# The input projection by seven products of halves, and attention beside the gates and the convolution's branch

## The chip, the cores and the metric

The kernel runs on one core of one Trainium2 chip. The time is the device time of one launch in microseconds (us), the median of the runs shown. The engines are named as in the profile: PE is TensorE's matmul, PEld its weight load, DVE VectorE, ACT ScalarE, POOL GpSimd, SP the queue that issues nearly all DMAs.

## The reference

One layer of a streaming encoder for 1024 prompt positions and 32 decoded ones, 1056 together, in float32:

```python
h = rmsnorm(x, g_mix);  proj = h @ w_in                     # 1024 -> 5120 columns
q, k, v, cb, cc, cx, ga, gc = split(proj)                   # 512 each; ga and gc 1024 each
z = q @ k.T / 8                                             # 8 heads of 64
a = sigmoid(z) * (product of 1 - sigmoid(z) over the keys between key and query), keys before the query only
y_attn = (a @ v) @ w_attn_out
conv_out = w[0] * u[t-2] + w[1] * u[t-1] + w[2] * u[t]      # u = cc * cx
y_conv = (cb * conv_out) @ w_conv_out
x = x + (sigmoid(ga) * y_attn + sigmoid(gc) * y_conv) @ w_o
x = x + square(relu(rmsnorm(x, g_ffn) @ w_up)) @ w_down
x = x + sigmoid(rmsnorm(x, g_ple) @ w_ple_gate) * (p @ w_ple);  y = rmsnorm(x, g_final)
```

k, v and the last two rows of u are outputs too. The 32 decoded positions attend to 256 cached keys as well.

## The kernel before

Activations lie with 128 features on the partitions and the 1056 positions along the row, 8 blocks of features for 1024. Each float32 operand is split into a high part that the matmul takes as it is (ACT copies it) and the rest (DVE subtracts), and a product is three matmuls: high by high, high by low, low by high (`gemm`, L102 to L108). The weight scale g_mix goes into x before the product, and the mean square of each position comes later: `rs`, one factor per position, multiplies each result of the input projection.

**The input projection** is 40 blocks of 128 columns. Each block is 3 tiles of 352 positions, and a tile ("group", one bank of PSUM) is 8 blocks of features by 3 matmuls of 352 columns. `first_unit` makes the blocks q0, k0 and v0 while x arrives, `qkv_unit`, `gate_unit` and `conv_unit` the others. `run_units` hands them out group by group.

**Attention** goes in 64 steps (p, j, i): 8 heads, and for each a round of 8 blocks of 128 queries; step i has i + 1 blocks of keys. Four stages of one step run in consecutive steps: `scores` (z on PE, two sigmoids on ACT, and on POOL a select that masks the last block of `r` and of `s`, L459), `weigh` (a running product over `r` on DVE, L467, and a multiply into `s`, L468), `flip` (transposes `pa` on PE, high part on ACT, low part on DVE, L498), `gather` (`av` on PE, L515, added on DVE, L523). Between these stages `fill` lets PE work on groups of the input projection: FILL of them in a round, spread by the number of keys of a step. In this part the order on each engine is the framework's scheduler's. Other parts (`tc.manual_schedule`) keep the order of the code.

**After attention** come the 12 blocks of the convolution (`conv_unit`), then 8 units of the convolution's branch ("oc"), 8 of attention's branch ("oa"), each 3 groups of 12 matmuls of 352, then 8 of w_o, and the MLP. A branch unit loads its gate from DRAM (`gd`), takes the sigmoid on ACT and multiplies it into the product as DVE reads it from PSUM; POOL adds the two branches (L666).

**w_up and w_down already go by seven products.** With two blocks of output columns, even and odd blocks of features and two halves of the positions, a product is a 2 by 2 matrix of blocks: weights A11 to A22, activations B11 to B22. Seven products of halves and sums of operands (S1 to S4 of the weights, T1 to T4 of the activations) take the place of eight. A "set" of w_up is two blocks of columns: 7 products x 2 quarters of 264 positions x 4 blocks of features x 3 matmuls = 168 matmuls of 264 columns, where two blocks by `gemm` are 2 x 3 x 8 x 3 = 144 matmuls of 352. POOL forms the sums of weights, and `run` and `side` interleave such steps with the products. w_up's code in line: `prepare_up`, `products` (L889 to L891), `up_set`.

SBUF has one pool of 34 tiles of a whole row (`blk`) for nearly everything.

## Time and profile before

| | us |
|---|---|
| median of 3 runs (1603.44 to 1609.71) | 1607.92 |
| the profiled execution: its own time | 1604.31 |
| its span, first to last instruction | 1602.6 |
| PE busy | 1564.4 (98%) |
| DVE busy | 996.3 (62%) |
| ACT busy | 671.0 (42%) |
| POOL busy | 328.1 (20%) |

The mean granted clock of PE is 0.993. Stages in the trace, from the span's start: the first matmul at 6.6 us, attention's first scores at 62.3 and its last `av` at 464.3, the convolution's branch from 596.6, attention's branch from 643.0, w_o from 689.3, w_up from 782.2, w_down from 1120.6, the last stage from 1478.0. A matmul's row gives a duration that overlaps with the next matmul's, so the cost of one in a dense stretch is the stretch's busy time over its count.

### The profile page before, as it was taken

How to read it: one execution, taken by the hardware profiler on the slowest of the kernel's cores; microseconds unless marked ns; L12 is line 12 of the kernel's file. 1: busy time of each engine (PE TensorE's matmuls, PEld its weight loads, DVE VectorE, ACT ScalarE, POOL GpSimd, SP SyncE). 2: the span in 40 equal slices, each digit the busy share in tenths (PEclk: the TensorE clock that was granted, in tenths of full speed). 3: DMA queues.
4: the chain of work that ended last, by engine and by line, in shares of the span. 5: the costliest groups of instructions: out<-in, count | busy, mean ns of one | idle time of the engine just before them, and what ended most of it. 6: DMA issues, size and time to landing. Idle time of an engine off the chain costs nothing.

```text
span 1602.6 us, 27656 instructions
## 1 busy us (share of the span) xinstructions
PE 1564.4 (98%) x11154; PEld 1547.2 (97%) x11154; DVE 996.3 (62%) x1386; ACT 671.0 (42%) x1105; POOL 328.1 (20%) x380
## 2 busy tenths in 40 slices
PE   8999999999999999999999999999999999998996
PEld 8999999999989999999989999999899999998996
DVE  4567676776544444565576555554478958897546
ACT  7344343444331114433355555555343344344443
POOL 0112222222220000321222222220011301022423
PEclk9999999999999999999999999999999999999998
DMA  7533242423111117433444443435877977752123
GB/s 309 192 97 117 74 143 76 124 95 100 61 67 42 39 33 250 161 120 127 149 169 148 148 147 134 144 141 189 292 259 234 312 253 232 244 181 80 50 80 135
DMA packets 99792, 238.39 MB, mean 149 GB/s; under 512 B 11824, under 2 KB 25776, under 8 KB 99664
## 3 DMA queue, kind: packets, MB, share of 16 engines
q1 hardware_dynamic: 99520, 236.60, 43.4%
q8 instruction: 87, 1.43, 0.4%
q14 instruction: 41, 0.34, 0.1%
q10 hardware_dynamic: 144, 0.03, 0.0%
HBM read 168.72 MB, written 63.68 MB: 145 GB/s over the span
## 4 chain that ended last, share of the span: by engine, by line
PE 80%; issue 6%; DVE 6%; DMA 2%; ACT 2%; POOL 2%; SPq 1%; POOLq 0%; DVEq 0%; ACTq 0%
PE ps_dn L1162 5%; PE ps_dn L1160 5%; PE ps_dn L1161 5%; PE ps_A L890 4%; PE ps_A L891 4%; PE ps_A L889 4%; PE ps_g L108 3%; PE ps_g L107 3%; PE ps_g L106 3%; PE ps_wo L107 2%; PE ps_wo L106 2%; PE ps_wo L108 2%; PE av L515 2%; PE ps_pg L106 2%; PE ps_S L890 2%
## 5 line engine op out<-in xcount | busy, mean ns | idle before, releaser
L1162 PE MATMUL ps_dn<-fh,wlo_dn 128*128 128x264 f32 x896 | 256.1, 286 | 3.3 <-DVE wlo_dn L1040 3.3
L1160 PE MATMUL ps_dn<-fh,whi_dn 128*128 128x264 f32 x896 | 255.9, 286 | 3.0 <-ACT whi_dn L1034 3.0
L1161 PE MATMUL ps_dn<-fl,whi_dn 128*128 128x264 f32 x896 | 255.3, 285 | 0.0
L1162 PEld LDWEIGHTS ps_dn<-fh,wlo_dn 128*128 128x128 f32 x896 | 169.3, 189 | 4.1 <-DVE wlo_dn L1040 4.1
L1160 PEld LDWEIGHTS ps_dn<-fh,whi_dn 128*128 128x128 f32 x896 | 169.4, 189 | 3.2 <-ACT whi_dn L1034 3.2
L1161 PEld LDWEIGHTS ps_dn<-fl,whi_dn 128*128 128x128 f32 x896 | 169.5, 189 | 0.0
L106 PE MATMUL ps_g<-xh,whi_g 128*128 128x352 f32 x384 | 127.3, 331 | 0.0
L107 PE MATMUL ps_g<-xl,whi_g 128*128 128x352 f32 x384 | 124.6, 324 | 0.0
L108 PE MATMUL ps_g<-xh,wlo_g 128*128 128x352 f32 x384 | 124.4, 324 | 0.0
L467 DVE TENSOR_TENSOR_SCAN r<-r 128x128 f32<-128x128 f32 (+3 forms) x64 | 87.6, 1370 | 34.9 <-POOL r L459 34.4
L1040 DVE TENSOR_TENSOR wlo_dn<-raw_dn,whi_dn 128x1024 fp32r<-128x1024 f32 x40 | 69.7, 1742 | 25.3 <-ACT whi_dn L1034 25.1
L876 POOL TENSOR_TENSOR s<-raw_u,raw_u 128x512 f32<-128x512 f32 x30 | 44.1, 1469 | 187.7 <-DVE slS L836 186.9
L451 ACT ACTIVATE r<-z 128x128 f32<-128x128 f32 (+3 forms) x64 | 41.9, 655 | 89.1 <-PE z L446 82.7
L1094 POOL TENSOR_TENSOR c<-c,rs 128x528 f32<-128x528 f32 x16 | 26.7, 1669 | 252.9 <-DVE c L1169 123.0
L1062 DVE TENSOR_TENSOR fl<-mr,fh 128x1056 fp32r<-128x1056 f32 x56 | 69.8, 1247 | 12.3 <-ACT fh L1057 12.3
L1034 ACT CAST whi_dn<-raw_dn 128x1024 fp32r<-128x1024 f32 x40 | 42.0, 1050 | 79.0 <-PE ps_dn L1161 78.6
L106 PEld LDWEIGHTS ps_g<-xh,whi_g 128*128 128x128 f32 x384 | 72.3, 188 | 0.3
L107 PEld LDWEIGHTS ps_g<-xl,whi_g 128*128 128x128 f32 x384 | 72.4, 189 | 0.0
L108 PEld LDWEIGHTS ps_g<-xh,wlo_g 128*128 128x128 f32 x384 | 72.2, 188 | 0.0
L890 PE MATMUL ps_A<-T,shS 128*128 128x264 f32 x240 | 68.4, 285 | 1.7 <-DVE T L776 1.7
L891 PE MATMUL ps_A<-T,slS 128*128 128x264 f32 x240 | 68.4, 285 | 0.0
L889 PE MATMUL ps_A<-B,whi_up 128*128 128x264 f32 x240 | 68.3, 285 | 0.0
(406 smaller groups left out, 4975.3 us busy)
## 6 DMA issues: line engine op xcount, KB each, us to landing
raw_dn<-in_w_down_dram SPq DMA_DIRECT2D x56, 512.0 KB, 4.5
mr<-mdT SPq DMA_DIRECT2D x32, 528.0 KB, 5.4
raw_u<-in_w_up_dram SPq DMA_DIRECT2D x32, 512.0 KB, 3.5
mdB<-m SPq DMA_DIRECT2D x48, 264.0 KB, 2.4
mr<-mdB SPq DMA_DIRECT2D x24, 528.0 KB, 6.0
gd<-sg SPq DMA_DIRECT2D x16, 528.0 KB, 2.7
mdT<-ta SPq DMA_DIRECT2D x32, 264.0 KB, 2.1
raw_g<-in_w_in_dram SPq DMA_DIRECT2D x16, 512.0 KB, 3.9
```

What stands on the lines that cost most here:

```text
L106: nc.tensor.matmul(ps, wh, xh[k][:, cols], start=(k == order[0]), stop=False)
L107: nc.tensor.matmul(ps, wh, xl[k][:, cols], start=False, stop=False)
L108: nc.tensor.matmul(ps, wl, xh[k][:, cols], start=False, stop=(k == order[-1]))
L467: nc.vector.tensor_tensor_scan(rev, rev, rev, 1.0, ALU.mult, ALU.bypass)
L889: nc.tensor.matmul(p_, wh[:, k, :], o[:, 0, c], start=new and n == 0, stop=False, **on)
L890: nc.tensor.matmul(p_, wh[:, k, :], o[:, 1, c], start=False, stop=False, **on)
L891: nc.tensor.matmul(p_, wl[:, k, :], o[:, 0, c], start=False, stop=z, **on)
L1040: dve(lo, raw, hi.bitcast(F32), op=sub)
L1062: dve(l, mraw.pop(v), opd[v].bitcast(F32), op=sub)
L1160: nc.tensor.matmul(ps, hi[:, j, :], oh, start=j == 0, stop=False)
L1161: nc.tensor.matmul(ps, hi[:, j, :], ol, start=False, stop=False)
L1162: nc.tensor.matmul(ps, lo[:, j, :], oh, start=False, stop=j == NP_ - 1)
```

## The change

The input projection goes first, as 14 "sets" of two blocks and 12 single gates. Sets 0 and 1 (4 gates) are plain products, made while x arrives (`first_gates`): 8 products of halves, in quarters of 264. The other 12 sets (cc, cx, cb, q, k, v, blocks 0 and 1; then q, k, v, cc, cx, cb, blocks 2 and 3) go by `seven`, now shared with w_up. `parts_x` and `sums_x` make B11 to B22 and T1 to T4 of the scaled x; `prepare` makes the weights' sums for the next set. What DVE did to a group as it read PSUM (times `rs`) is a step behind the set: `follow` starts generators that scale (`scaled`), split, transpose, convolve and write to DRAM while the next set's products run. Queries, keys, values and the convolution's result now all go through DRAM (`qd`, `kd`, `vd`, `cvd`); `keys_values` loads keys and values for a round one round ahead.

Then attention runs. Its `fill` is now 12 gates (groups of 24 matmuls of 264) and after them the convolution's branch (groups of 12 matmuls of 352), 7.25 groups in a round and not 9.6. A gate leaves PSUM by ACT, unscaled; when a branch unit loads it, POOL multiplies it by `rs` (`branch_unit`, L783 in the changed kernel), ahead of the sigmoid. POOL's addition of the two branches moves to DVE. The decoded positions' attention moves from behind the last step to steps 3, 6 and 9. Behind attention stands what is left of the convolution's branch, attention's branch and w_o as before.

```diff
-GATES = (3, 3, 3, 7)
-FILL = 9.6
+AT_IN = (4, 8, 10, 12, 14, 18)
+PLAIN_GATES = 4
+FILL = 7.25
 FILL_BASE = 2.0
 ORDER = "SAFLBFG"
-START = 9
+START = 6
...
+    def seven(s_, m1, m2, last, after=None):
...
+        for t, a, b in q:
+            x[t] = product("A11", "B11", t)
+            nc.scalar.copy(p1[t], x[t])
+            yield
+        for t, a, b in q:
+            z[t] = product("S1", "T1", t)
+            nc.scalar.copy(s5[t], z[t])
+            yield
+        for t, a, b in q:
+            product("S2", "T2", t, x[t])
+            nc.scalar.copy(u2[t], x[t])
+            yield
+        for t, a, b in q:
+            dve(m1[:, a], product("A12", "B21", t), p1[t], op=add)
+            yield
+        done("11")
+        for t, a, b in q:
+            product("S3", "T3", t, x[t])
+            dve(m2[:, b], x[t], s5[t], op=sub)
+            yield
+        done("22")
+        for t, a, b in q:
+            product("S4", "B22", t, z[t])
+            dve(m1[:, b], u2[t], z[t], op=sub)
+            yield
+        done("12")
+        for t, a, b in q:
+            product("A22", "T4", t, x[t])
+            last(m2, a, x[t])
+            yield
+            if t == 0:
+                done("near")
+        done("21")
...
+    SETS = [("g", 0), ("g", 2)] + [(nm, 0) for nm in ("cc", "cx", "cb", "q", "k", "v")]
+    SETS += [(nm, 2) for nm in ("q", "k", "v", "cc", "cx", "cb")]
+    base = {"g": goff, "q": 0, "k": 4, "v": 8, "cb": coff, "cc": coff + 4, "cx": coff + 8}
...
-    first_raw = {"q": raw_w(w_in, 0, KD, "q0")}
-    load_x(0)
-    first_raw["k"] = raw_w(w_in, 4, KD, "k0")
-    load_x(1)
-    load_x(2)
+    near_, far_, whole_ = slice(0, TQ), slice(TQ, TH), slice(0, TH)
+    n_ = base["g"]
+    raws["i0"] = [raw_w(w_in, n_, KD, "i0_0")]
+    load_x(0, near_)
+    raws["i0"].append(raw_w(w_in, n_ + 1, KD, "i0_1"))
+    load_x(0, far_)
+    load_x(1, whole_)
...
+    def keys_or_queries(nm, p, m):
+        scaled(m, HD**-0.5 if nm == "q" else None)
+        yield
+        d = [qd[p, :, i, :] if nm == "q" else kd[p, i] for i in range(2)]
+        h = blk(f"{nm}h{p}", F32R, [P, SEQ])
+        nc.scalar.copy(h, m[:, :SEQ])
+        nc.scalar.copy((qsT if nm == "q" else ksT)[p], m[:, SEQ:])
+        nc.sync.dma_start(d[0], h.bitcast(F32))
+        if nm == "k":
+            nc.sync.dma_start(k_out[p], m)
+            for _ in range(4):
+                yield
+        yield
+        l = m[:, :SEQ]
+        dve(l.bitcast(F32R), l, h.bitcast(F32), op=sub)
+        nc.sync.dma_start(d[1], l)
...
+            nc.sync.dma_start(vd[p, j], vs.bitcast(F32).rearrange("p a c -> p (a c)"))
...
+    def scaled(m, by=None):
+        if by is None:
+            dve(m, m, rs, op=ALU.mult)
+        else:
+            nc.vector.scalar_tensor_tensor(m, m, by, rs, op0=ALU.mult, op1=ALU.mult)
...
+    def conv_in(nb, m):
+
+        scaled(m)
+        yield
+        u = cst["cc", nb]
+        dve(u, u, m, op=ALU.mult)
...
+        y = cst["y", nb] = blk(f"yc{nb}")
+        nc.scalar.activation(y, u, AF.Copy, scale=w2)
...
+        mix(y[:, 1:], u[:, : T - 1], w1, y[:, 1:], add)
...
+    def conv_gate(nb, m):
+        scaled(m)
+        yield
+        dve(m, m, cst.pop(("y", nb)), op=ALU.mult)
+        yield
+        h = blk(f"cvh{nb}", F32R)
+        nc.scalar.copy(h, m)
+        nc.sync.dma_start(cvd[nb, 0], h.bitcast(F32))
+        yield
+        dve(m.bitcast(F32R), m, h.bitcast(F32), op=sub)
+        nc.sync.dma_start(cvd[nb, 1], m)
...
+    def follow(nm, n, ms, wait=0):
+        gens = []
+        for p, m in zip((n, n + 1), ms):
+            if nm in "qk":
+                gens.append(keys_or_queries(nm, p, m))
+            elif nm == "v":
+                gens.append(values(p, m))
+            elif nm == "cc":
+                cst["cc", p] = m
+                gens.append(call(scaled, m))
+            else:
+                gens.append({"cx": conv_in, "cb": conv_gate}[nm](p, m))
...
-                nc.vector.tensor_tensor(sg[:, ts[t]], ps, rs[:, ts[t]], op=ALU.mult)
+    def gate_group(n, w, sg, t):
+        c = t // 2 + 1
+        ps = products(f"g{n}_{t}", ((w[0], f"B1{c}"), (w[1], f"B2{c}")), quarters[t % 2])
+        nc.scalar.copy(sg[:, quarters[t]], ps)
...
+    def keys_values(p, j):
+        kk = st["k", p, j] = blk(f"ks{p}{j}", F32R, [P, SEQ])
+        for i in range(2):
+            nc.sync.dma_start(kk[64 * i : 64 * i + 64, :].bitcast(F32), kd[p, i, 64 * j : 64 * j + 64, :])
+        vv = st["v", p, j] = blk(f"vv{p}{j}", F32R, [P, 8, P])
+        nc.sync.dma_start(vv.bitcast(F32).rearrange("p a c -> p (a c)"), vd[p, j])
...
     def branch_unit(nm, n, ww, bh, bl):
         def load():
             sg = blk(f"s{nm}{n}")
-            return sg, load_w(ww, n, 4, f"o{nm}{n}")
+            nc.sync.dma_start(sg, gd[n + (8 if nm == "c" else 0)])
+            w = load_w(ww, n, 4, f"o{nm}{n}")
+            pool(sg, sg, rs, op=ALU.mult)
+            nc.scalar.activation(sg, sg, AF.Sigmoid)
...
             if nm == "a" and not last:
-                nc.gpsimd.tensor_tensor(m, m, sg, op=ALU.add)
+                dve(m, m, sg, op=add)
...
-    units = [first_unit()]
-    g_of = GATES
-    g = 0
-    for p in range(4):
-        units += [gate_unit(n) for n in range(g, g + g_of[p])]
-        g += g_of[p]
-        if p < 3:
-            units += [qkv_unit(p + 1, nm) for nm in "qkv"]
-    units += [gate_unit(n) for n in range(g, 16)]
-    units += [conv_unit(nb, nm) for nb in range(4) for nm in ("cc", "cx", "cb")]
-    work = run_units(units, 1)
+    units = [gate_unit(n) for n in range(PLAIN_GATES, 14)] + [last_gates(14)]
+    units += [branch_unit("c", n, w_conv_out, ch, cl) for n in range(KD)]
+    work = run_units(units)
...
+        run(first_gates())
+        for s_ in range(2, len(SETS)):
+            nm, n = SETS[s_]
+            if s_ == 2:
+                side.append(after(1, stats_x()))
+            if s_ + 1 < len(SETS):
+                side.append(prepare(f"i{s_ + 1}", AT_IN))
+            else:
+                side.extend([after(4, second_parts(0)), after(6, second_parts(1)), after(7, call(next, work))])
+            if s_ + 2 < len(SETS):
+                side.append(after(5, call(fetch_in, s_ + 2)))
+            m = blk(f"m1_i{s_}"), blk(f"m2_i{s_}")
+            run(seven(f"i{s_}", *m, copy_of))
+            follow(nm, n, m, 6 * (s_ == 2))
+        keys_values(0, 0)
+        run(ahead(START))
...
-    units = [branch_unit("c", n, w_conv_out, ch, cl) for n in range(KD)]
     units += [branch_unit("a", n, w_attn_out, oh, ol) for n in range(KD)]
     units += [wo_unit(n) for n in range(KD)]
-    run_all(units)
```

How the order moved, at three places. On DVE, what belongs to the convolution's inputs. Before, in the stretch behind attention (`ps_cx`, `ps_cb`: groups in PSUM; `u`: cc times cx; `yc`: the convolution's sum; `wlo_cc`: the next block's weights' low part):

```order
L389 TENSOR_TENSOR cx_5559<-ps_cx_0_5560,rs 128x352
L389 TENSOR_TENSOR cx_5559<-ps_cx_1_5586,rs 128x352
L389 TENSOR_TENSOR cx_5559<-ps_cx_2_5612,rs 128x352
L399 TENSOR_TENSOR u_5638<-cc_5474,cx_5559 128x1024
L400 TENSOR_TENSOR u_5638<-cc_5474,cx_5559 128x32
L98 TENSOR_TENSOR wlo_cc_5653<-raw_cc_5650,whi_cc_5652 128x1024
L407 SCALAR_TENSOR_TENSOR yc_5646<-u_5638,vecT,yc_5646 128x1058
L389 TENSOR_TENSOR cb_5656<-ps_cb_0_5657,rs 128x352
```

Now, in the set of cb behind that of cx (`m_i`: results of a set, `slS`: a weights' sum's low part for the next set, `ps_A12i`, `ps_A11i`: products):

```order
L454 TENSOR_TENSOR m_i_1020<-m_i_1020,rs 128x1056
L239 TENSOR_TENSOR m_i_1287<-ps_A12i_1_1431,p_i_1290 128x264
L505 TENSOR_TENSOR m_i_761<-m_i_761,m_i_1020 128x1056
L244 TENSOR_TENSOR m_i_1288<-ps_A11i_0_1295,s_i_1293 128x264
L153 TENSOR_TENSOR slS_i_1470<-raw_i_1_1165,shS_i_1468 128x512
L244 TENSOR_TENSOR m_i_1288<-ps_A11i_1_1318,s_i_1294 128x264
L142 SCALAR_TENSOR_TENSOR yc_1463<-m_i_761,vecT,yc_1463 128x1055
```

The scaling of a whole row, the convolution and the weights' low parts now stand between the reads of PSUM.

On DVE in attention. Before, at the end of a round and the start of the next (`sg<-ps_g`: a gate leaves PSUM; the running product over `r` is printed here as SCALAR_TENSOR_TENSOR):

```order
L498 TENSOR_TENSOR at_2724<-pa_2827,at_2723 128x2x128
L468 TENSOR_TENSOR s_2810<-s_2810,r_2811 128x1023
L366 TENSOR_TENSOR sg_2838<-ps_g_0_2839,rs 128x352
L467 SCALAR_TENSOR_TENSOR r_2873<-r_2873 128x128
L468 TENSOR_TENSOR s_2872<-s_2872,r_2873 128x127
L498 TENSOR_TENSOR at_2881<-pa_2884,at_2880 128x4x128
```

Now, in a round of the last two heads:

```order
L700 SCALAR_TENSOR_TENSOR r_7356<-r_7356 128x1024
L758 TENSOR_TENSOR oT_7237<-av_7338,avl_7347 64x256
L731 TENSOR_TENSOR at_7295<-pa_7363,at_7294 128x4x128
L801 TENSOR_TENSOR mg_7315<-ps_oc_1_7370,sc_7162 128x352
L701 TENSOR_TENSOR s_7355<-s_7355,r_7356 128x1023
L731 TENSOR_TENSOR at_7297<-pa_7386,at_7296 128x2x128
L801 TENSOR_TENSOR mg_7315<-ps_oc_2_7391,sc_7162 128x352
L99 TENSOR_TENSOR wlo_oc_7489<-raw_oc_7486,whi_oc_7488 128x512
```

In the last two heads' rounds DVE reads the branch's groups, which before stood behind attention; in the earlier rounds it reads no group at all, since ACT does.

On POOL in the same part of attention. Before, selects and memsets alone:

```order
L459 AFFINE_SELECT r_4921<-r_4921 128x128
L459 AFFINE_SELECT s_4920<-s_4920 128x128
L504 MEMSET at_4931 128x128
L459 AFFINE_SELECT r_5025<-r_5025 128x128
L459 AFFINE_SELECT s_5024<-s_5024 128x128
```

Now, with the gates' multiply by `rs` between them (`sc`: a gate loaded for the convolution's branch):

```order
L692 AFFINE_SELECT r_7356<-r_7356 128x128
L692 AFFINE_SELECT s_7355<-s_7355 128x128
L783 TENSOR_TENSOR sc_7305<-sc_7305,rs 128x1056
L692 AFFINE_SELECT r_7413<-r_7413 128x128
L692 AFFINE_SELECT s_7412<-s_7412 128x128
L737 MEMSET at_7422 128x128
L737 MEMSET at_7423 128x128
L692 AFFINE_SELECT r_7461<-r_7461 128x128
L692 AFFINE_SELECT s_7460<-s_7460 128x128
L737 MEMSET at_7524 128x128
L783 TENSOR_TENSOR sc_7484<-sc_7484,rs 128x1056
```

Seven of the sixteen multiplies stand between selects of the last three rounds, the others behind them.

More of the change, by code (lines that the diff above doesn't have):

```diff
@@ new lines, in products @@
+    def products(name, terms, c, p_=None):
+        new = p_ is None
+        if new:
+            p_ = group(f"ps_{name}", TQ)
+        n = 0
+        for (wh, wl), b in terms:
+            for k in range(4):
+                o, z = oper[b][k], n == 4 * len(terms) - 1
+                on = dict(skip_group_check=not new)
+                nc.tensor.matmul(p_, wh[:, k, :], o[:, 0, c], start=new and n == 0, stop=False, **on)
+                nc.tensor.matmul(p_, wh[:, k, :], o[:, 1, c], start=False, stop=False, **on)
+                nc.tensor.matmul(p_, wl[:, k, :], o[:, 0, c], start=False, stop=z, **on)
+                n += 1
+        return p_
@@ new lines, in after, with call, run @@
+    def after(n, *gens):
+        for _ in range(n):
+            yield
+        for g in gens:
+            yield from g
+    def call(f, *a):
+        f(*a)
+        yield
+    def run(body):
+        for _ in body:
+            for g in list(side):
+                if next(g, g) is g:
+                    side.remove(g)
+    goff = (3 * SB + 3 * CW) // P
+    coff = 3 * SB // P
+    SETS = [("g", 0), ("g", 2)] + [(nm, 0) for nm in ("cc", "cx", "cb", "q", "k", "v")]
+    SETS += [(nm, 2) for nm in ("q", "k", "v", "cc", "cx", "cb")]
@@ L697, in row_rms @@
+    for p in range(4):
+        h, l = split(oT[p], f"o{p}")
+        oh.append(h)
+        ol.append(l)
+    c_att.close()
+    gps2 = ctx.enter_context(tc.tile_pool(name="gps2", bufs=4, space=PSUM))
+    c_mlp = ExitStack()
+    fpool = wpool[0] = c_mlp.enter_context(tc.tile_pool(name="fpool", bufs=2))
+    pools[:] = [gps2, gps, gps2]
     def row_rms(src, r9, blocks, name, square=False):
@@ L1488 @@
     data = {
[L1489 removed]
+        "xf": x.T.reshape(KD, P, T),
         "xr_": x,
```

855 lines of the change are left out of this document (407 added, 448 removed).

## The prediction

> **What bounds the kernel now.** I began with the page's busy shares over 40 slices, to see which engine has no slack.
>
> ```profile
> PE   8999999999999999999999999999999999998996
> DVE  4567676776544444565576555554478958897546
> POOL 0112222222220000321222222220011301022423
> PEclk9999999999999999999999999999999999999998
> ```
>
> PE is full from the second slice on, at the full granted clock; DVE has a third to a half of each slice free, POOL more. Then the stretches by windows (the columns are the stretch in us, its length, then busy time and instructions of PE, PEld, DVE, ACT and POOL, the granted clock, the DMA share and GB/s): attention, attention's branch, and some 15 sets of w_up.
>
> ```profile
> 62.00:464.00 402.00, 398.94 (x2621) 388.70 (x2621) 268.08 (x377) 161.09 (x295) 96.19 (x197) 1.00 0.32 103
> 643.00:689.00 46.00, 46.00 (x288) 46.00 (x287) 24.44 (x38) 19.07 (x21) 18.79 (x7) 1.00 0.46 155
> 806.00:1110.00 304.00, 300.85 (x2458) 299.78 (x2457) 171.46 (x254) 165.39 (x317) 76.85 (x56) 1.00 0.43 152
> ```
>
> Attention idles PE for 402.00 - 398.94 = 3.1 us, attention's branch not at all, w_up for 3.2 of 304. PE's waits name what little is lost:
>
> ```profile
> PE ps_q L106 <- ACT xh L161: 6.6, 1, 6.6
> PE ps_A L890 <- DVE T L776: 1.7, 1, 1.7
> PE pas L602 <- DVE ss L468: 1.7, 1, 1.7
> ```
>
> The largest is the program's start. So the time is PE's work, and a change is worth the PE time it removes, less the idle time it opens. For the price of a matmul I also read the starts of two stages of equal matmuls (minimum, median and maximum duration, then first and last start):
>
> ```profile
> L106 PE MATMUL ps_oa<-o0h,whi_oa x24: 322/323/323, 643.0 to 687.4; 128*128 128x352 f32 x24
> L106 PE MATMUL ps_wo<-mh,whi_wo x192: 318/323/330, 689.3 to 781.8; 128*128 128x352 f32 x192
> ```
>
> A matmul of 352 columns costs (689.3 - 643.0) / 288 = 160.8 ns, one of 264 columns, by the window of w_up, 300.85 / 2458 = 122.4 ns.
>
> **The change part by part.** *Products.* Two blocks of queries, keys, values or convolution inputs cost 144 x 0.1608 = 23.16 us now, a set 168 x 0.1224 = 20.56. That is -2.59, and 12 sets give **-31.1**. The 16 gates stay plain but go in quarters: two of them are 192 x 0.1224 = 23.50 for 23.16, +0.35, and 8 pairs give **+2.8**. Sum for PE: -28.3.
>
> The Trainium skill, "TensorE: Matmul & The Clock Gate", section "Back-to-back issue gap", has a rule against all of this: a sustained stream spaces matmuls of 128 columns about 81 ns apart and of 512 about 131, so narrow ones pay a large fixed part. An estimate on its straight line is 99 ns for 264 columns and 110 for 352, and the sum would be about +33, not -28. The trace disagrees with it (122.4 and 160.8, in dense stretches), and the rows decide.
>
> *The start* is plain products as before, in smaller loads of x: the first wait of 6.6 stays, and later parts may come a little sooner or later. Between -1 and +3; I take 0.
>
> *Work behind a set.* A group was scaled as DVE read it from PSUM; now a whole row is scaled in SBUF, split and convolved while the next set runs. The fullest set is that of cb, behind cx. Its rows:
>
> ```profile
> L836 DVE TENSOR_TENSOR slS<-s,shS 128x512 fp32r<-128x512 f32 x45 | 33.6, 746 | 39.7 <-ACT shS L834 39.7
> L98 DVE TENSOR_TENSOR wlo_up<-raw_u,whi_up 128x1024 fp32r<-128x1024 f32 x16 | 19.4, 1214 | 2.4 <-ACT whi_up L97 2.4
> L959 DVE TENSOR_TENSOR m<-ps_A,p 128x264 f32<-128x264 f32 x29 | 12.4, 428 | 16.0 <-PE ps_A L891 16.0
> L632 DVE TENSOR_TENSOR ml<-mg,mh 128x1056 fp32r<-128x1056 f32 x7 | 8.8, 1258 | 15.7 <-ACT mh L631 15.7
> L407 DVE SCALAR_TENSOR_TENSOR yc<-u,vecT,yc 128x1058 f32<-128x1058 f32 x6 | 7.9, 1316 | 1.7 <-ACT yc L405 1.7
> ```
>
> DVE: 6 reads of PSUM x 0.43, 5 low parts x about 0.7 and one of 1.2 for the next set's weights, 2 scalings and 2 products for u at 1.26 each by the row `ml`, 4 passes of the convolution x 1.32, small ones 0.7: 18.3 of PE's 20.56. In w_up it was 171.46 / 15 = 11.4 a set, with 3.15 / 15 = 0.2 us of PE idle each. Sets behind q, k, v need 12 to 14. There are two cx sets and two cb sets; only these are near the limit, and POOL's sums of weights (below) can push them over: 0 to +8, I take **+1.5**.
>
> *DVE and POOL hold each other up.* The timeline and the groups:
>
> ```profile
> 300.62 1.79 POOL L459 TENSOR_SCALAR_AFFINE_SELECT s<-s 128x128 f32<-128x128 f32 x1 [0.62 <-ACT s L451]
> 300.03 2.29 DVE L467 TENSOR_TENSOR_SCAN r<-r 128x1024 f32<-128x1024 f32 x1
> ...
> 854.30 1.63 POOL L876 TENSOR_TENSOR s<-raw_u,raw_u 128x512 f32<-128x512 f32 x1 [0.69 <-DVE slS L836]
> 854.81 1.69 DVE L907 TENSOR_TENSOR m<-m,m 128x528 f32<-128x528 f32 x1
> ...
> L459 POOL TENSOR_SCALAR_AFFINE_SELECT s<-s 128x128 f32<-128x128 f32 x64 | 63.0, 984 | 20.7 <-ACT s L451 20.4
> L459 POOL TENSOR_SCALAR_AFFINE_SELECT r<-r 128x128 f32<-128x128 f32 x64 | 22.6, 354 | 219.8 <-ACT r L451 216.6 <-DMA raw_k<-in_w_in_dram 3.0
> L666 POOL TENSOR_TENSOR mg<-mg,sa 128x1056 f32<-128x1056 f32 x7 | 20.0, 2854 | 116.4 <-DVE sa L660 113.0 <-ACT sa L645 3.4
> L876 POOL TENSOR_TENSOR s<-raw_u,raw_u 128x512 f32<-128x512 f32 x30 | 44.1, 1469 | 187.7 <-DVE slS L836 186.9 <-DMA raw_u<-in_w_up_dram 0.7
> ```
>
> The same select takes 0.29 us beside an idle DVE (r mean 354) and 1.79 beside a scan, ending as the scan does; a DVE operation of 0.7 us takes 1.69 beside a POOL sum and ends 0.57 after it. So a POOL operation of two rows in SBUF costs DVE its time, and the reverse. The change puts 16 such operations in (a gate times `rs`, 128x1056, 2.85 us by L666): 7 among the last rounds' selects, one behind them and 8 in attention's branch; it takes out 7 additions from there.
>
> The Trainium skill says so in "SBUF — State Buffer", section "SBUF: two separate sides": the shared ports are a lock held for a whole instruction. The trace agrees (1.79 against 0.29). By this rule each multiply stops DVE's two-input work entirely; that is the second rival below, and I count a part of it here.
>
> *Attention.* The rows of PE and DVE there, and below the dots two of the branches, which now come in part under it:
>
> ```profile
> L494 PE MATMUL pa<-ident,s 128*128 128x128 f32 x288 | 46.6, 275 | 1.1 <-POOL at L504 0.8 <-POOL s L459 0.3
> L515 PE MATMUL av<-at,vs 128*128 128x256 f32 x316 | 43.5, 284 | 0.9 <-DVE at L498 0.9
> L445 PE MATMUL z<-ks,q 128*128 128x384 f32 (+4 forms) x96 | 33.1, 347 | 0.0
> L446 PE MATMUL z<-ks,q 128*128 128x384 f32 (+4 forms) x96 | 32.9, 344 | 0.9 <-DMA q<-qd 0.9
> L467 DVE TENSOR_TENSOR_SCAN r<-r 128x128 f32<-128x128 f32 (+3 forms) x64 | 87.6, 1370 | 34.9 <-POOL r L459 34.4
> L498 DVE TENSOR_TENSOR at<-pa,at 128x512 fp32r<-128x512 f32 (+2 forms) x96 | 50.8, 542 | 1.4 <-ACT at L497 1.3
> L468 DVE TENSOR_TENSOR s<-s,r 128x127 f32<-128x127 f32 (+3 forms) x64 | 48.1, 753 | 3.0 <-POOL s L459 0.9
> L523 DVE TENSOR_TENSOR oT<-av,avl 64x256 f32<-64x256 f32 x31 | 12.8, 414 | 15.9 <-ACT avl L522 15.6
> ...
> L658 DVE TENSOR_TENSOR mg<-ps_oc,sc 128x352 f32<-128x352 f32 x24 | 12.0, 520 | 10.2 <-PE ps_oc L108 7.3 <-ACT sc L645 3.0
> L98 DVE TENSOR_TENSOR wlo_oa<-raw_oa,whi_oa 128x512 fp32r<-128x512 f32 x8 | 5.5, 684 | 0.0
> ```
>
> Attention's own are 796 matmuls (and 27 of values, moved); the other 1798 of 2621 are input blocks at 0.1608, which leaves 398.94 - 289.1 = 109.8 us, 13.7 a round. DVE's own rows sum to 199.3, at most 24.9 a round. A round had 9.6 x 24 x 0.1608 = 37.0 of other products, 50.7 in all: DVE had slack twice over. A round of gates now has 7.25 x 24 x 0.1224 = 21.3, so 35.0, against DVE's 24.9 plus two low parts of weights of 1.21, 27.3: still PE's, at 78%. In the round that has the convolution's branch alone it is 7.25 x 12 x 0.1608 = 14.0, so 27.7, while DVE has 24.9 + 7.25 x 0.52 (its reads of PSUM) + 2.4 x 0.69 (low parts of the units' weights) = 30.4: 2.7 us over without the multiplies, 10 with 2.6 of them (7 in 2.7 rounds). The last round has the units that are left on PE to cover it (0 to +6), and its end waits for the last flips, gathers and splits, with few matmuls left beside it (2 to 4); the other rounds lose what they lost before or some more (1 to 2). That is 6 to 22; I take 12, as the multiplies will often meet selects or reads of PSUM and not scans, less the 3.1 of before: **+9**, between +3 and +19. Queued behind a late scan are the multiply into `s`, the flips and the branch's reads of PSUM, for which PE waits within a few groups.
>
> *Transfers.* Keys and values (0.5 MB of each a round: 128 rows of 1024 floats) are now loaded from DRAM a round ahead, on SP behind the weights; 1 MB in 35 us is 29 GB/s, beside the 103 that attention's window moves at a share of 0.32. The convolution's results come back the same way. I cost this at 0; if a round's keys were late, PE would wait as it did for `q<-qd` in the row of L446, 0.9, once a round: 7.
>
> *Attention's branch.* A unit is 36 x 0.1608 = 5.79 on PE. DVE reads 3 x 0.52, a low part of weights 0.69 and the split 1.26, and now adds the branches itself, 1.25: 4.8. POOL's addition (2.85) becomes a multiply (2.85), but it stands ahead of the sigmoid, which the reads of PSUM wait for. Between 0 and +15 (4.8 + 2.85 = 7.65 is 1.86 over, 8 times); the gates are loaded a unit ahead, so I take **+2**.
>
> Behind w_o's start nothing changes. Total -31.1 + 2.8 + 0 + 1.5 + 9 + 2 = **-15.8**. On the profiled execution, 1604.31, that is 1588.5; the median shown lies 3.6 above it, so 1592.
>
> **The rivals.** *PE bound throughout.* DVE's slack takes it all, as it does in w_up: -28.3 or a little less; 1604.3 - 28 = 1576, median 1580. For it: 46.00 busy of 46.00 with POOL's additions beside it. Against: the round at 30.4 on DVE for 27.7 on PE.
>
> *The lock decides in attention's last rounds.* Every multiply there blocks DVE where it has no slack: +20 in attention (7 x 2.85) and +5 in its branch, so -28.3 + 1.5 + 20 + 5 = -2, median 1606, between 1600 and 1615: no change. For it: DVE in the branch's round is over 100% before the first multiply. Against: only 2.7 of 8 rounds have it.
>
> *Sets start late.* A set's seven products need five sums of weights, each by a load, POOL (by the row of L876 above, 2 of 1.47 a set; two other sums at no more than that each make 5.9), ACT and DVE, inside 20.56 us, and results, rows waiting for their split, x's parts and weights share 34 buffers. If DVE at 18.3 with POOL's 5.9 in its way (24.2) passes the delay on to the next set's sums, each of 12 sets starts late. At 3.6 us each (24.2 - 20.56) it is -15.8 + 12 x 3.6 = +27, median 1635; slower than 1616 from about 2 us each. For it: it is the densest stretch of DVE in the kernel. Against: only four sets are so full, and w_up runs such sets with 0.2 us lost each.
>
> **How the numbers follow.** A measurement of this kernel can tell 0.5%, 8 us, from no change: faster is below 1600, slower above 1616. My forecast (-10 to -22) 0.48, PE throughout 0.19, the lock 0.20, late sets 0.13; in this 0.01 is for matmuls of 264 columns that come wider spaced in the sets than in w_up. Faster is 0.48 + 0.19 = 0.67, same 0.20, slower 0.13. The range leaves out late sets and the ends of the two others: 1578 to 1610. The time is the forecast's, 1592.
>
> **What would show it.** Right: in the sets 168 matmuls in 20.6 us and PE idle under 5 us in all twelve; attention about 289 us from its first scores to its last `av`, DVE at 90% or more in the last three rounds, with scans beside multiplies longer than elsewhere, and PE's waits there on DVE; attention's branch from about 625, w_up from about 766. Wrong: waits of PE on low parts of weights' sums at each set's start (late sets), PE over 98% in the last rounds (PE throughout), or a spacing of 264 columns above 125 ns in the sets.

## The result, and the profile after

The changed kernel takes 1634.05 us (median of 4 runs, 1631.26 to 1636.45) where the kernel before takes 1608.76 (4 runs too): a ratio of 1.0164, 95% interval 1.0133 to 1.0194. It is slower by 25 us; the forecast was 1592, between 1578 and 1610. The profiled execution took 1636.45 us, its span 1634.7, 32.1 more than before.

The page's busy shares over 40 slices, as shown of before:

```profile
PE   8999999989999888989999999999899999998996
DVE  7568565745776688775667555554488968897446
POOL 1213233022333434311312222221010301022423
PEclk9999999999999989999999999999999999999998
```

PE is no longer full in slices 9, 14 to 16 and 18 (29 lies in w_down, which the change left alone), and in slice 15 its granted clock falls. Slices 14 to 16, 531 to 654 us, are the last rounds of attention; DVE is busy there for 6, 8 and 8 tenths and POOL for 3 to 4, its most. Slice 9 holds attention's start, 18 the start of w_o. The windows, with the columns explained above: sets, two halves of the first 78 us of attention, its middle, its last three stretches, attention's branch, w_o.

```profile
140.00:300.00 160.00, 160.00 (x1312) 159.94 (x1312) 96.52 (x126) 67.02 (x142) 43.30 (x28) 1.00 0.44 162
333.00:372.00 39.00, 30.78 (x209) 26.76 (x208) 20.37 (x31) 17.29 (x39) 13.43 (x35) 0.91 0.46 153
372.00:411.00 39.00, 37.79 (x287) 35.91 (x285) 22.11 (x31) 17.21 (x37) 11.02 (x21) 0.91 0.36 109
411.00:530.00 119.00, 113.41 (x888) 109.25 (x888) 83.53 (x109) 65.77 (x135) 39.96 (x77) 1.00 0.33 101
530.00:570.00 40.00, 36.13 (x274) 34.24 (x272) 26.97 (x34) 20.39 (x43) 15.95 (x27) 1.00 0.64 218
570.00:612.00 42.00, 34.36 (x206) 32.07 (x206) 37.19 (x52) 23.00 (x46) 16.79 (x32) 0.88 0.34 102
612.00:657.00 45.00, 37.57 (x242) 35.07 (x242) 38.99 (x50) 24.52 (x42) 17.60 (x24) 0.96 0.20 60
667.00:714.00 47.00, 47.00 (x294) 46.86 (x292) 39.52 (x45) 19.85 (x22) 18.58 (x8) 1.00 0.42 143
714.00:811.00 97.00, 92.77 (x576) 92.32 (x576) 57.16 (x69) 30.26 (x38) 22.54 (x11) 1.00 0.46 161
```

The sets run as forecast: 160.00 / 1312 = 122.0 ns a matmul, without a stop. Attention does not. From 333 to 657 us PE sits idle 8.2 + 1.2 + 5.6 + 3.9 + 7.6 + 7.4 = 34 us, where attention had lost 3.1; and the clock costs more, because behind some stops PE works at half speed for some us (rows below). The mean clocks give 39 x 0.09 + 39 x 0.09 + 42 x 0.12 + 45 x 0.04 = 14 us. PE's busy time there, 290.0, less 14 is 276. The prediction's 289 us for attention hold 12 of idle time, so 277 of work: the work was right. PE's waits, and the starts of attention's branch and of w_o:

```profile
PE pa L727 <- DVE at L731: 14.7, 14, 5.2
PE av L748 <- DVE at L731: 8.8, 9, 2.3
PE pa L727 <- DVE oT L758: 7.9, 3, 4.7
```

```profile
L107 PE MATMUL ps_oa<-o0h,whi_oa x24: 318/322/327, 667.4 to 711.7; 128*128 128x352 f32 x24
L107 PE MATMUL ps_wo<-mh,whi_wo x192: 317/322/328, 713.7 to 810.5; 128*128 128x352 f32 x192
```

Against before, attention's branch starts 24.4 us later and w_o 24.4; w_o then takes 97.3 us (to 811.0, the start of w_up) where it took 92.9. The rest of the 32.1 lies behind w_up's start (3.3), where nothing was changed; the runs below spread by as much in that part.

The first stop of 5.2 us and the clock behind it, by windows of 3 and 4 us:

```profile
356.00:360.00 4.00, 0.00 (x0) 0.00 (x0) 3.46 (x4) 0.50 (x2) 3.92 (x8) 0.97 0.18 36
360.00:363.00 3.00, 2.02 (x10) 2.02 (x11) 3.00 (x5) 0.59 (x1) 0.80 (x2) 0.50 0.01 3
363.00:366.00 3.00, 3.00 (x12) 2.65 (x12) 2.09 (x3) 0.90 (x3) 0.00 (x0) 0.50 0.00 0
366.00:369.00 3.00, 3.00 (x24) 2.90 (x23) 1.45 (x1) 2.76 (x6) 0.85 (x2) 0.91 0.02 5
```

PE runs nothing, then 12 matmuls in 3 us at a clock of 0.50, then 24. Just before the stop POOL and DVE work on the decoded positions, and the round's own selects and scans come behind that.

A piece of the timeline shows what happens where the branch's gates meet attention:

```profile
567.53 2.35 DVE L700 TENSOR_TENSOR_SCAN r<-r 128x1024 f32<-128x1024 f32 x1 [0.18 <-POOL r L692]
568.04 4.05 POOL L783 TENSOR_TENSOR sc<-sc,rs 128x1056 f32<-128x1056 f32 x1 [0.29 <-DMA sc<-gd]
569.99 3.18 DVE L701 TENSOR_TENSOR s<-s,r 128x1023 f32<-128x1023 f32 x1
573.20 0.42 DVE L758 TENSOR_TENSOR oT<-av,avl 64x256 f32<-64x256 f32 x1
573.67 0.69 PE L727 MATMUL pa<-ident,s 128*128 128x128 f32 x2 [4.67 <-DVE oT L758]
...
602.29 2.58 POOL L783 TENSOR_TENSOR sc<-sc,rs 128x1056 f32<-128x1056 f32 x1 [1.28 <-DMA sc<-gd]
602.51 4.51 DVE L700 TENSOR_TENSOR_SCAN r<-r 128x1024 f32<-128x1024 f32 x1
```

The multiply takes 4.05 beside a scan; DVE's multiply behind it takes 3.18 (1.22 in the run with DVE scaling below), ending 1.1 after POOL's; the read of `av` queued behind that is late, and PE stops 4.67 us. At 602 it is the scan that takes 4.51 instead of 2.3.

### The profile page after: what moved, and what is told of

Read it like the earlier page. It is cut to its first block, busy times and chain, and to the rows that moved or that the text cites. A ratio compares the mean times of both kernels' runs of the same rounds, so it can differ in the third digit from the quotient of the medians.

```text
span 1634.7 us, 29582 instructions
## 1 busy us (share of the span) xinstructions
PE 1558.3 (95%) x11826; PEld 1534.7 (94%) x11826; DVE 1090.6 (67%) x1444; ACT 762.2 (47%) x1358; POOL 414.9 (25%) x417
## 4 chain that ended last, share of the span: by engine, by line
PE 78%; DVE 10%; issue 4%; ACT 3%; DMA 2%; POOL 1%; SPq 0%; DVEq 0%; POOLq 0%; ACTq 0%
PE ps_dn L1309 5%; PE ps_dn L1307 5%; PE ps_dn L1308 5%; PE ps_A11u L204 3%; PE ps_A11u L203 3%; PE ps_A11u L205 3%; PE ps_g L205 3%; PE ps_g L204 3%; PE ps_g L203 3%; PE ps_A11i L205 3%; PE ps_A11i L203 3%; PE ps_A11i L204 3%; PE av L748 2%; DVE r L700 2%; PE ps_wo L108 2%
## 5 line engine op out<-in xcount | busy, mean ns | idle before, releaser
L203 PE MATMUL ps_g<-B,whi_g 128*128 128x264 f32 x384 | 112.7, 293 | 0.0
L205 PE MATMUL ps_g<-B,wlo_g 128*128 128x264 f32 x384 | 110.7, 288 | 0.0
L204 PE MATMUL ps_g<-B,whi_g 128*128 128x264 f32 x384 | 110.5, 288 | 0.0
L190 POOL TENSOR_TENSOR s_u<-raw_u,raw_u 128x512 f32<-128x512 f32 x30 | 44.2, 1472 | 188.4 <-DVE slS_u L153 187.8
L190 POOL TENSOR_TENSOR s_i<-raw_i,raw_i 128x512 f32<-128x512 f32 x24 | 32.7, 1361 | 192.2 <-DVE slS_i L153 154.6
L205 PEld LDWEIGHTS ps_g<-B,wlo_g 128*128 128x128 f32 x384 | 73.2, 191 | 0.5 <-issue 0.5
L204 PEld LDWEIGHTS ps_g<-B,whi_g 128*128 128x128 f32 x384 | 73.1, 190 | 0.5 <-issue 0.5
L203 PEld LDWEIGHTS ps_g<-B,whi_g 128*128 128x128 f32 x384 | 73.3, 191 | 0.1
L727 PE MATMUL pa<-ident,s 128*128 128x128 f32 x288 | 50.0, 290 | 22.6 <-DVE at L731 14.7
L204 PE MATMUL ps_A11u<-T,shS_u 128*128 128x264 f32 x240 | 68.6, 286 | 1.6 <-DVE T L147 1.6
L203 PE MATMUL ps_A11u<-T,shS_u 128*128 128x264 f32 x240 | 68.2, 284 | 0.0
```

What stands on the lines that cost most here:

```text
L190: f()
L203: nc.tensor.matmul(p_, wh[:, k, :], o[:, 0, c], start=new and n == 0, stop=False, **on)
L204: nc.tensor.matmul(p_, wh[:, k, :], o[:, 1, c], start=False, stop=False, **on)
L205: nc.tensor.matmul(p_, wl[:, k, :], o[:, 0, c], start=False, stop=z, **on)
L727: nc.tensor.transpose(pt[:, b, :], s[:, (b0 + b) * P : (b0 + b + 1) * P], ident)
```

## The experiments

Each is one edit to the changed kernel or to another run, timed on the same chip in turn with the kernel before (1606.7 to 1607.7 in the four sessions).

**The decoded positions' attention behind the last step.**

```diff
-        if j == 1 and c == 0:
-            nc.scalar.copy(oT[p][:, SEQ:], osT[:, p, :])
...
-        if n in (3, 6, 9):
+        if n >= len(steps):
             next(sample)
...
+        nc.scalar.copy(oT[p][:, SEQ:], osT[:, p, :])
```

The copies of its results move behind the last step with it.

> One edit to the changed kernel (1634 us): the decoded positions' attention goes back behind the last step instead of steps 3, 6 and 9. Theory P (placement): the 8.2 us of PE idle between 333 and 372 us, and the half clock that follows, belong to that piece of work, which waits for its cached keys and then fills POOL while PE has no group left to run; the time falls by 6 to 12 us, PE idles 3 us or less in attention's first 39 us at a granted clock of 1.00, and 2 to 4 us come back behind the last step. Theory C (cover): the first round is short of PE work whatever stands in it; the idle time stays within 2 us of 8.2 and the time within 3 us of 1634.

1630.1 us, ratio 1.0143 (1.0124 to 1.0162): 3.9 less than the changed kernel, which is not clear of noise (the intervals overlap). Its first round, and its end:

```profile
333.00:372.00 39.00, 36.50 (x285) 35.02 (x286) 25.89 (x35) 22.39 (x47) 13.70 (x29) 1.00 0.44 130
612.00:664.00 52.00, 42.81 (x252) 38.15 (x253) 33.47 (x44) 17.95 (x35) 18.52 (x27) 0.84 0.24 78
```

The first round loses 2.5 where it lost 8.2, at clock 1.00, so that idle time did belong to this piece. Up to 530 us PE idles 10.6, at clock 1.00, where the changed kernel idled 15.0. But the end loses more than there (7.4 at 0.96): 9.2 idle, at a clock of 0.84. The placement moved most of a loss rather than made it. Theory P has the cause of the first stop right and the gain too large.

**Gates scaled by DVE.**

```diff
-        nc.scalar.copy(sg[:, quarters[t]], ps)
+        nc.vector.tensor_tensor(sg[:, quarters[t]], ps, rs[:, quarters[t]], op=ALU.mult)
...
-            pool(sg, sg, rs, op=ALU.mult)
+            if nm == "a" and n < PLAIN_GATES:
+                pool(sg, sg, rs, op=ALU.mult)
```

> One edit to the changed kernel: 12 of the 16 gates are scaled by rs as DVE reads them from PSUM (0.45 us per quarter, 48 quarters, in place of ACT's copies), so POOL multiplies only the four gates made first, all of them behind attention. Theory L (lock): the multiplies stretch scans and multiplies of DVE (4.51 us for a scan of 2.2, 3.18 for a multiply of 1.2) and so stop PE and its clock; scans of 1024 stay below 2.5 us, the 18.9 us of PE idle between 530 and 656 us fall below 10, its clock there to 0.98 or more, and the time falls by 12 to 20 us. Theory D (DVE is full in the branch's rounds without POOL): at most 5 us faster, and PE's waits there stay on the same tiles.

1607.6 us, ratio 1.0002 (0.9991 to 1.0014): 26.4 less, more than theory L had. Attention's windows and the scans of 1024 from 530 to 657 us:

```profile
333.00:530.00 197.00, 184.43 (x1404) 175.06 (x1402) 141.90 (x209) 88.80 (x177) 67.27 (x135) 0.97 0.36 110
530.00:612.00 82.00, 76.13 (x539) 71.34 (x540) 68.14 (x105) 46.75 (x92) 26.47 (x63) 1.00 0.55 177
...
L700 DVE TENSOR_TENSOR_SCAN r<-r 128x1024 f32<-128x1024 f32 x3 | 7.0, 2318 | 1.6 <-POOL r L692 1.5
```

Scans are back at 2.3 and the clock holds at 1.00 in the last rounds. w_o takes 92.7 again (696.1 to 788.8), so the multiplies in attention's branch had cost 4.6 there. What stays is 12.6 idle in the first 197 us, with the clock at 0.97, and 8.6 idle in the 127 behind: 21 from the first scores to the last `av`, where the kernel before has 3.

**Gates alone beside attention.**

```diff
-FILL = 7.25
+FILL = 5.25
```

> One number of the changed kernel: 5.25 groups a round for 7.25, so that attention runs beside gates alone and the convolution's branch stands behind it, dense. Theory T (thin rounds of the branch): attention's last three rounds are the loss; PE's idle time there falls by 8 or more and the time by 5 to 12 us. Theory C (cover is thin everywhere): a gate round is now 13.7 + 15.4 = 29.1 us of PE for at least 27 of DVE, so idle time spreads over all eight rounds; the time stays within 4 us or rises by up to 10.

1620.5 us, ratio 1.0091 (1.0074 to 1.0108), 13.5 less, a little more than theory T's range. It doesn't settle T against the lock, since with the branch all but one of the seven POOL multiplies also leave attention. The time goes against theory C, but a stretch without a multiply shows that thin cover costs something too:

```profile
411.00:450.00 39.00, 36.14 (x279) 34.03 (x278) 29.72 (x42) 21.47 (x47) 13.48 (x29) 1.00 0.40 117
450.00:490.00 40.00, 36.81 (x284) 35.27 (x283) 31.00 (x42) 24.21 (x50) 14.16 (x32) 1.00 0.34 107
490.00:530.00 40.00, 35.31 (x269) 33.02 (x268) 31.96 (x41) 23.90 (x46) 16.86 (x30) 1.00 0.32 97
```

PE idles 10.7 here. In the same 119 us the changed kernel idles 5.6, and so does the run with DVE scaling (6.0), though its DVE is as busy as here (92.5 us for 92.7): DVE's share does not make the difference. The loss doesn't grow evenly with thinner cover, for with 6.25 groups (below) it is 5.6 again.

**Both of the first two:** samples with `n >= len(steps)`, gates by `nc.vector.tensor_tensor(..., rs[...])`.

> The edits of the first two runs together. If placement and lock are separate causes, the gains add: 18 to 32 us less than the changed kernel, which is between 1602 and 1616. If cover is what is short, the sum is at most 8 us less, above 1626.

1609.0 us, ratio 1.0014 (1.0004 to 1.0025). The gains don't add: nothing beyond DVE scaling. The first round idles 2.5 at clock 1.00, and the last 40 us stand at 0.87.

**A multiply of POOL that nothing waits for.** To the run with DVE scaling:

```diff
+            if nm == "c":
+                m = blk(f"mg{n}")
+                mg.append(m)
+                pool(m, rs, rs, op=ALU.mult)
             nc.scalar.activation(sg, sg, AF.Sigmoid)
...
+            m = mg[n]
```

> The run in which DVE scales the gates (1607.6 us), and beside it a multiply of the old size on POOL for each of the eight units of the convolution's branch, of rs by rs into the unit's still empty result: it waits for no load, and the sigmoid does not wait for it. Theory L (lock): what the multiplies cost is the time in which POOL holds DVE; scans beside them take 4 us and more again, and 10 to 25 us come back, 1618 to 1633. Theory W (their waits: selects queued behind a multiply that waits for its gate's load, and the sigmoid behind it): at most 4 us come back.

1612.7 us, ratio 1.0032 (1.0020 to 1.0043): 5.1 come back, between the two theories. The multiplies were shorter (1.95 at the median) and met shorter operations of DVE: no scan took above 2.5, but the weighs together 54.5 us where they had taken 48.3, one of them 2.53. So this run shows that a multiply on POOL costs something even when nothing waits for it; as a measure of the real ones it was not good enough.

**Twice the cover.** To the run with DVE scaling:

```diff
+        products(f"x{n}_{t}", ((w[0], f"B1{c}"), (w[1], f"B2{c}")), quarters[t % 2])
         ps = products(f"g{n}_{t}", ((w[0], f"B1{c}"), (w[1], f"B2{c}")), quarters[t % 2])
...
                 gemm(ps, wo, 0, bh, bl, ts[t])
+                if nm == "c":
+                    ps = group(f"ps_x{nm}{n}_{t}")
+                    gemm(ps, wo, 0, bh, bl, ts[t])
```

> The same run with DVE scaling, and every group of the 12 gates and of the convolution's branch multiplied twice (the first result is thrown away): 48 x 2.94 + 24 x 1.93 = 187.4 us more for PE, about 35 a round where there were 19. It computes the same result. Theory C (cover): what PE still loses in attention, 21 us of idle time and some 10 us by the half clock, is for want of other work between dependent steps; PE idles 8 us or less from the first scores to the last av, at a clock of 1.00, and the time is 1764 to 1776 instead of 1795. Theory O (the order of queues loses it whatever stands beside it): idle time stays within 5 us of 21 and the time within 8 us of 1795.

1771.4 us (2 runs, 1767.4 to 1775.5), as theory C had it: 24 less than the added work would make. Attention from the first scores to the last `av`:

```profile
349.00:781.00 432.00, 425.75 (x3288) 415.85 (x3288) 237.95 (x342) 151.83 (x293) 102.25 (x207) 1.00 0.27 85
```

PE idles 6.3 in eight rounds, at clock 1.00. The same code with the same queues on DVE, ACT and POOL loses its time only when a round has some 19 us of other products and not when it has 39. (DVE's share falls with it, to 55%.)

**Decoded positions in long steps, and 6.25 groups.** To DVE scaling:

```diff
+            kks.append(kk)
+        yield
...
-        if n in (3, 6, 9):
+        if n in (1, 13, 21, 29):
             next(sample)
```

The piece that loads the cached keys is split off as one of its own, and the copies of the results stand behind the last step again.

> DVE scaling as above, and the decoded positions' attention in four pieces at the sixth step of the rounds (its cached keys loaded in the second step of all), where a step has the most groups beside it. Theory P (the pieces lose time by their place): 5 to 9 us less than 1607.6, no half clock before 420 us. Theory M (moved is not saved, as in the run with the edits of the first two): within 3 us of 1607.6.

1605.6 us, ratio 0.9987 (0.9974 to 1.0000), 2.1 less than DVE scaling: theory M, moved is not saved. With fewer groups beside it:

```diff
-FILL = 7.25
+FILL = 6.25
```

> The edits of the run before it, and 6.25 groups a round for 7.25. If the branch's rounds are still the thin ones, 2 to 5 us less than it; if every round is short of cover, 0 to 5 us more.

1603.8 us, ratio 0.9985 (0.9973 to 0.9997). 1.8 less, no more than the sessions spread; theories can't be told apart by it. Without POOL's multiplies it matters little how much of the branch stands beside attention.

**POOL's multiplies, everything else as with DVE scaling.** The changed kernel with DVE's copy in ACT's place:

```diff
-        nc.scalar.copy(sg[:, quarters[t]], ps)
+        nc.vector.tensor_copy(sg[:, quarters[t]], ps)
```

> The changed kernel with one difference: DVE, not ACT, copies the 12 gates out of PSUM, unscaled; POOL multiplies all 16 by rs as in the change. Against the run with DVE scaling (1607.6) it differs by POOL's multiplies alone, now with their chain: a multiply waits for its gate's load, the selects queue behind it on POOL, and ACT's sigmoid, with the casts and copies queued behind it, waits for it. Theory Q (queues): the chain makes up what the idle multiplies (5.1 us) left unexplained of 26; the time is 1624 to 1636 and ACT's late copies of av show in DVE's waits (10 us or more above 14). Theory E (ACT's relief by evicting on DVE was the gain): the time is 1606 to 1616.

1628.5 us, ratio 1.0133 (1.0103 to 1.0162). So of the 26.4 us, 20.9 came by the absence of 12 multiplies (DVE's reads of PSUM take 427 ns in both runs). The 5.5 that are left, for evicting on DVE instead of ACT, are not clear of noise: the intervals overlap. Theory Q has the time, but not its own sign: DVE waits for ACT's copies of `av` 14.2 us, as with DVE scaling (13.6). What differs is DVE's own length. The groups of weighs, of DVE scaling and then of this run:

```profile
L701 DVE TENSOR_TENSOR s<-s,r 128x127 f32<-128x127 f32 (+3 forms) x64 | 48.3, 758 | 2.1
```

```profile
L701 DVE TENSOR_TENSOR s<-s,r 128x127 f32<-128x127 f32 (+3 forms) x64 | 58.7, 922 | 2.2 <-POOL s L692 0.4
```

The weighs are 10.4 us longer, the scans 2.0 (89.4 against 87.4). Five of the seven multiplies in attention met a weigh and one a scan: POOL turns to its multiply right behind the selects, and that is when DVE scans and weighs. A rival would be that the selects themselves come late, queued behind a multiply on POOL; but DVE waits for them 25.5 us here and 24.8 with DVE scaling, so that adds next to nothing.

**The same multiplies on DVE.** To the run before:

```diff
-            pool(sg, sg, rs, op=ALU.mult)
+            dve(sg, sg, rs, op=ALU.mult)
```

> The run in which DVE copies the gates (1628.5 us), with the 16 multiplies by rs on DVE instead of POOL: the same operation at the same place, with the same wait for the gate's load ahead of it and the sigmoid behind it, but it can't hold DVE against POOL; DVE has 16 x 1.25 us more. Theory L (lock, and where it falls): the time is 1608 to 1616, and no weigh or scan of DVE takes more than 2.5 us between 540 and 660 us. Theory Q (the chain of load, multiply and sigmoid): the loads now stop DVE itself, and the time is 1624 to 1640.

1609.4 us, ratio 1.0009 (0.9991 to 1.0026): 19.1 less than with POOL, though DVE does 16 operations of 1.26 us more, each behind the same load and ahead of the same sigmoid. Theory L. The weighs are back at 757 ns:

```profile
L701 DVE TENSOR_TENSOR s<-s,r 128x127 f32<-128x127 f32 (+3 forms) x64 | 48.2, 757 | 1.4
L783 DVE TENSOR_TENSOR sc<-sc,rs 128x1056 f32<-128x1056 f32 x8 | 10.2, 1275 | 0.3 <-DMA sc<-gd 0.2
```

**Four more edits to the run with 6.25 groups**, for a better kernel. The first:

```diff
-START = 6
-FILL = 6.25
+START = 3
+FILL = 6.75
```

> The best so far (1603.8: DVE scaling, samples in long steps, 6.25 groups a round), with 3 groups ahead of attention in place of 6 and 6.75 a round: 1.5 us more cover in each round. If cover per round is what is short, 2 to 6 us less; if the last sets' rows are late without the six groups, 0 to 6 us more.

1609.5 us (1.0010, 0.9994 to 1.0025): 5.7 more, 4 by the ratios, whose intervals just touch. Scores begin at 324.5 instead of 332.8, but attention's branch at 648.2 instead of 644.0. Half a group more in each round brought no gain; what cost the rest is open.

```diff
-ORDER = "SAFLBFG"
+ORDER = "SFAFLFBFG"
```

> The same best, with the groups of a step handed out at three places between its stages in place of two (behind the scores as well). If PE's waits on the flips come from stages that stand too close together, 2 to 5 us less; if from too little work in all, within 2 us.

1605.5 us (0.9991, 0.9978 to 1.0005): no gain, as too little work in all would have it.

The third starts the second block's share of cx's following work 8 products into the set, not 6:

```diff
-        side.extend([after(wait, gens[0]), after(wait + (6 if nm in ("v", "cx") else 1), gens[1])])
+        side.extend([after(wait, gens[0]), after(wait + {"v": 6, "cx": 8}.get(nm, 1), gens[1])])
```

> The same best, with the second block's part of cx's following work two products later in cb's set. The stop of 2.7 us at 126 us and the half clock behind it were DVE held by four POOL sums in a row while it was behind; if the overlap of this work with POOL's sums decides, both go and the time falls by 3 to 5 us; if DVE is simply full in that set, they stay.

1603.2 us (0.9981, 0.9967 to 0.9996), the lowest measured, but only 0.6 under the run it was made from, which is noise. The window, first of the run it was made from, then of this one:

```profile
120.00:140.00 20.00, 17.30 (x129) 17.09 (x129) 19.04 (x20) 7.90 (x15) 6.70 (x4) 0.92 0.24 96
```

```profile
120.00:140.00 20.00, 17.18 (x139) 16.76 (x138) 18.95 (x19) 8.53 (x17) 7.26 (x4) 1.00 0.25 100
```

The half clock behind the stop is gone, the stop of 2.8 us is not. The edit can't be credited with that: in four other runs whose sets are those of the changed kernel (gates alone, POOL's idle multiplies, twice the cover, the multiplies on DVE) the same stop of 2.7 has clock 1.00 behind it too, and the next run, which has this edit, has 0.91 in the window. So the expectation failed: the stop stays, and the half clock comes and goes from run to run. The stop itself stands at 134 us, not at 126; at 126 DVE falls behind.

The fourth, made from the third, hands out groups of the branch in the three steps behind the last scores:

```diff
+            elif op == "F" and n >= len(steps):
+                fill(min(done + 2, 72))
```

> The best so far (1603.2: DVE scaling, samples in long steps, 6.25 groups, cx later), and in each of the three steps behind the last scores four groups of the branch that stood behind attention. If the end of attention loses PE time for want of work in its last stages (up to 5.0 us of one wait of av), 2 to 6 us less; if those waits are DVE's own length, within 2 us.

1606.1 us (0.9994, 0.9980 to 1.0008): no gain, and the wait of `av` at 5.1 as before (5.0). More groups behind the last scores do not shorten it.

## Why the prediction was wrong

By its own steps, against the profiled execution (1636.45, forecast 1588.5, missed by 48):

- **Products, -28.3: right.** A set's matmul took 122.0 ns for the 122.4 reckoned. PE's work in attention came to 276 us at full clock, as the sum had it. Matmuls of 264 columns were no wider spaced in the sets than in w_up, and the sums by 122.4 and 160.8 held. The Trainium skill, "TensorE: Matmul & The Clock Gate", section "Back-to-back issue gap", gives 81 ns for 128 columns and 131 for 512; by the estimate on that line the change would have cost 33 us, and the traces disagree with it.
- **Work behind a set, +1.5: small.** One stop of 2.7 us at 134 us with a half clock behind it, some 4 in all, inside the bounds of 0 to 8, in the set of cb as named. Ten us ahead of it the timeline has four POOL sums in a row, of which these are the first and the last, and beside them two low parts of 0.7 that take 3.40 and a scaling of 2.34 instead of 1.25:

```profile
124.49 1.28 POOL L190 TENSOR_TENSOR s_i<-raw_i,raw_i 128x512 f32<-128x512 f32 x1 [17.68 <-DVE slS_i L153]
124.62 3.40 DVE L153 TENSOR_TENSOR slS_i<-s_i,shS_i 128x512 fp32r<-128x512 f32 x2
127.94 2.34 DVE L454 TENSOR_TENSOR m_i<-m_i,rs 128x1056 f32<-128x1056 f32 x1
129.24 2.19 POOL L190 TENSOR_TENSOR s_i<-s_i,raw_i 128x512 f32<-128x512 f32 x1
```

- **Attention, +9 between +3 and +19: this failed.** Idle time and half clock made 48 us, less the 3 of before: 45, so 36 of the 48 missed are here. Two sentences of that step were wrong, and one term was not in it. The first took "still PE's, at 78%" to mean that a round of gates loses 1 to 2 us for six rounds together. From 333 to 530 us, ahead of the first multiply, PE lost 15 of idle and 7 by the clock. Some half of these 22 belong to the decoded positions' piece, for which the sum had no term: with it behind the last step the stretch lost 10.6 at clock 1.00, though most of the difference came back at the end. The rest goes with the cover. A share of 78% says that DVE can do the work in the time. It does not say that each flip and weigh is done when PE comes to it: in the traces PE stops for one though groups of other products follow in its order. That takes other products between dependent steps, and the change took almost half of them away, from 37 to 21 us a round. Twice the cover brought the idle time of all eight rounds down to 6 us, and 5.25 groups for 7.25 took that of one stretch from 5.6 to 10.7. The second sentence put multiplies beside "selects or reads of PSUM and not scans"; in the run with DVE's copies six of seven met scans and weighs.
- **Half clock: missing from the prediction.** It counted idle time and not what can follow a stop, as in the windows from 356 to 369. In attention this added 14 us to 34 of idle.
- **Attention's branch, +2 between 0 and +15:** its own 46.3 us did not grow, but w_o behind it did, by 4.4. The price showed a stage later than reckoned; DVE scaling, without the last four multiplies, took it away. The first low part of w_o's weights, beside the last multiplies:

```profile
L99 DVE TENSOR_TENSOR wlo_wo<-raw_wo,whi_wo 128x1024 fp32r<-128x1024 f32 x1 | 3.5, 3468 | 0.0
```

- What is left, some 7 us, is the 3.3 behind w_up's start, and 3 to 4 in the start, the groups ahead of attention and roundings, which no run took apart.

Of the rivals, *the lock decides in attention's last rounds* had the right mechanism and nearly the price: +20 and +5 forecast for 15 multiplies, 20.9 measured for 12, of which the profiles have 14.7 ahead of attention's branch (664.2 against 649.5) and 4.8 in w_o. Its row was in the profile of before. The Trainium skill, "SBUF — State Buffer", section "SBUF: two separate sides", has a lock on the shared ports that is held for a whole instruction; the trace agrees (DVE's multiply of 3.18 ends 1.1 us after POOL's of 4.05). The rival's time, 1606, was not measured: the kernel without 12 of the multiplies stands at 1607.6, but that is chance. The result is slower because the lock came on top of the thin cover, and the cover alone, with the smaller terms, eats the 28 us. *Sets start late* named the right sign for a wrong reason: the sets are the part that worked.

How far the multiply's chain of waits adds to the lock is not fully settled: POOL's idle multiplies cost 5.1, but were shorter and fell elsewhere. That the same chain on DVE costs next to nothing (1609.4 for 1607.6) speaks for the lock and the place where it falls.

## What to carry to other kernels

Work that stands between the dependent steps of a pipeline is worth more than its own time: making it cheaper or moving it out uncovers the waits it hid, so reckon a stage also by what stands between two dependent steps of the slowest queue, not by the engines' shares alone. A POOL operation on SBUF is not free beside a DVE that is short of time; put it where DVE reads PSUM anyway (here a factor that had been free in the read became 16 operations), or on DVE itself. And a PE stop of some us costs its length and can cost a stretch of half speed behind it.

## What was not expected of the hardware

The same POOL multiply (128x1056) took 2.46 us or 4.05 and lengthened DVE's neighbour by up to 2.2 us, and where it met neither a weigh nor a scan (617 us) it lengthened none: its price is set by what it meets, and an order that issues it right behind the selects made it meet a weigh or a scan six times in seven. DVE took 16 multiplies at 1.26 us each with less loss than POOL with 16 at 2.6 "beside" it. And the same stop of 2.7 or 2.8 us (at 134 us) had a half clock behind it in 10 of the 15 traces that have it, and full clock in 5, without any edit that accounts for it: in these traces a stop of this length may or may not cost the clock.
